# Rows of the last two experts placed by TensorE, an earlier reload of the running sum, and stores on two queues, in a diffusion backbone layer

## The chip, the cores and the metric

One core of one Trainium2 chip runs the whole layer as one program. Times are device microseconds of one execution. A profiled execution gives the span, from the first to the last instruction, and the trace behind all rows shown here. The engines are TensorE (PE in the profile; PEld is its weight load), VectorE (DVE), ScalarE (ACT), GpSimd (POOL) and SyncE (SP, which only issues transfers here). A name with a q behind it (SPq) is the engine's instruction queue.

## The reference, cut to what matters

```python
x = x + mx[2] * yx                                     # first residual
x = x + mx[5] * hier_moe(modulate(x, norm2_g, ...))    # 16 experts, top 2 inside the top group
return rmsnorm(x, final_g)

def hier_moe(h, ...):          # t: 512 tokens x 1024
    gates = ...                # (512, 16), two entries of a row are not zero
    for e in range(16):
        he = silu(t @ w1[e]) * (t @ w3[e])             # 1024 -> 512, twice
        out = out + gates[:, e:e + 1] * (he @ w2[e])   # 512 -> 1024
```

All data are float32. A token goes to two of the 16 experts. The last step is a norm over the 1024 values of each token, scaled by `final_g`.

## The kernel before, in words

The experts take the second half of the time. For each of them up to 96 tokens (CAP) are gathered from a table `td` in DRAM by an indirect transfer of GpSimd's queue, turned by TensorE (`columns`), multiplied by w1 and w3 (`up_`), gated (`gated` on ScalarE, `hidden` on VectorE), turned again (`hidden_t`), multiplied by w2 (`down`), scaled by the gate (`rows`, on VectorE) and added to the tokens' rows of `yd`, a running sum in DRAM, by a scatter that adds (`add_rows`, an indirect transfer of GpSimd's queue). A part behind the main path, under `tc.If(nmax > CAP)`, repeats the work for experts with more than 96 tokens. It is not entered in this run.

Weights come in 192 pieces of 512 KB, 12 for an expert, into a ring of 34 slots. Each piece is split into two reduced parts, a high one (a copy by ScalarE) and a low one (a subtraction by VectorE that overwrites the slot), and each product is made of three (`mm3`). `used()` counts a piece as consumed, and issues the load 33 pieces ahead on SyncE and the split six pieces ahead on ScalarE and VectorE. The order of each engine's instructions is that of the program text (`manual_schedule`): every engine takes its own list in order and waits for the others by semaphores.

Expert 15 has no scatter. A 0/1 matrix that says which of its 96 rows belongs to which token is made on VectorE at expert 8 (`OH0`, four tiles of 128 tokens), turned by TensorE and kept as `oT`. At the end `final_parts` splits the scaled rows into a high and a low part, and `placed` multiplies them by `oT` into eight PSUM banks (four tiles of 128 tokens, two halves of 512 columns). `final_loads` reads the sum `yd` back into four tiles; `added` adds the banks to it (VectorE for tiles 0 to 2; for tile 3 TensorE adds the sum into the bank by a product with the identity). `squared` (ScalarE) sums the squares, `rooted` and `root` make the factor for two tiles at a time, `done` scales, and `store` writes a half tile as two transfers of 64 partitions, since a tile holds rows of two runs of the output. For tiles 0 to 2 the product with `final_g` is made by GpSimd (`by_g`), and `done` multiplies by the factor alone. The reads of `final_loads` stand in the program behind the scatter of expert 14, which they need. The slots that the last norm uses (`fr`) are those of the ring that would come after the last piece.

Nine products on a spare bank (`mm(bank[7]...)`) stand in TensorE's list between the placing and the additions of tile 3. The table for the square root is loaded by a small ScalarE instruction (`warm`) ahead of the last products.

Of the kernel before, what the change touches and what calls it, by code (L numbers as in the profile page):

```python
# [9 lines left out]
BF = mybir.dt.bfloat16  # L10
# [4 lines left out]
CAP = 96  # L15
# [3 lines left out]
def layer_kernel(  # L19
# [18 lines left out]
    def dap(t, off, dims):  # L38
        return bass.AP(tensor=t.tensor, offset=t.offset + off, ap=dims)
# [26 lines left out]
    def atr(kb, shape, part=128):  # L66
        return at(kb, shape, part, F32R)

    def f32(a):
        return a.bitcast(F32)  # L70
# [11 lines left out]
    def nb(g="w"):  # L82
        b = bank[groups[g][bctr[g] % len(groups[g])]]
        bctr[g] += 1
        return b
# [4 lines left out]
    def mm(o, l, r, start, stop):  # L90
        T.matmul(o, l, r, start=start, stop=stop)  # L91
# [104 lines left out]
    def tr(o, i, n=None):  # L196
        n = i.partition_size() if n is None else n
        T.transpose(o, i, ident[0:n, 0:n])  # L198
# [1168 lines left out]
    def gated(e):  # L1367
        S.activation(at(sil, [512], part=CAP), st["h", e, 0][0:CAP], AF.Silu)  # L1368
# [27 lines left out]
    def rows(e, hs=(0, 1)):  # L1396
        if e < 0:
            return
        yb = st["y", e]
        yt = at(YO if e < 15 else XG, [1024], part=CAP)  # L1400
        for h in hs:
            r = slice(h * 512, h * 512 + 512)
            V.scalar_tensor_tensor(yt[:, r], yb[h][0:CAP], gate[:, e:e + 1], mx5[h][0:CAP], op0=OP.mult, op1=OP.mult)  # L1403
        if e < 15:
            add_rows(yt, idx[:, e:e + 1])


# [13 lines left out]
    ab = tables()  # L1421


    fr = [ring[(len(pieces) + q) % len(ring)] for q in range(12)]
    yL_ = [at(fr[q], [1024]) for q in range(4)]
    fg = at(fr[4], [1024])
    yH, yl = atr(fr[5], [1024], part=CAP), atr(fr[6], [1024], part=CAP)
    yf = [at(fr[8 + q], [1024]) for q in range(4)]
    ss3 = ct([128, 2, 4], F32, "ss3")
    rs3 = ct([128, 4], F32, "rs3")  # L1430
# [6 lines left out]
        for i in range(4):  # L1437
            D.dma_start(yL_[i], yd[i * 128:(i + 1) * 128, :])

    def final_parts(h):  # L1440
        yt, r = at(XG, [1024], part=CAP), half[h]
        S.activation(yH[:, r], yt[:, r], AF.Copy)
        V.tensor_sub(yl[:, r], yt[:, r], f32(yH[:, r]))

    def placed(h):
        for i in range(4):
            b = st["f", i, h] = nb()
            mm(b, oT[:, i], yH[:, half[h]], True, False)
            mm(b, oT[:, i], yl[:, half[h]], False, (i, h) not in by_pe)

    by_pe = ((3, 0), (3, 1))

# [8 lines left out]

    def squared(i, h):
        S.activation(at(fr[7], [512]), total(i, h), AF.Square, accum_out=ss3[:, h, i:i + 1])  # L1463

    def by_g(i, h):
        P.tensor_mul(yf[i][:, half[h]], yL_[i][:, half[h]], fg[:, half[h]])

    def rooted(q):

# [12 lines left out]

    def store(i, y, r):
        for j in range(2):
            D.dma_start(dap(out, (2 * i + j) * 1024 + r.start, [[8192, 64], [1, r.stop - r.start]]), y[j * 64:(j + 1) * 64, r])

    def done(i, h, e):
        r, c = half[h], slice(i, i + 1)
        if e is V:
            V.scalar_tensor_tensor(yf[i][:, r], total(i, h), rs3[:, c], fg[:, r], op0=OP.mult, op1=OP.mult)  # L1490
        elif e is D:
            V.tensor_scalar(yf[i][:, r], yf[i][:, r], rs3[:, c], None, op0=OP.mult)  # L1492
        elif e is S:
            S.activation(yf[i][:, r], yf[i][:, r], AF.Copy, scale=rs3[:, c])
        else:
            P.tensor_scalar(yf[i][:, r], yf[i][:, r], rs3[:, c], None, op0=OP.mult)
        store(i, yf[i], r)

    load_to(len(ring) - 1)
    oT = atr(195, [4, 128], part=CAP)  # L1500
    if True:
        split_to(AHEAD - 1)
        up_(0, 0, 0)
        used()
        up_(0, 0, 1)
        used()
        up_(0, 0, 2)
        slots(*ab)
        gather(1)
        counts()  # L1510
        used()
        up_(0, 0, 3)
        used()
        up_(0, 1, 0)
        gated(0)
        used()
        up_(0, 1, 1)
        used()
        up_(0, 1, 2)
        used()  # L1520
        up_(0, 1, 3)
        hidden(0)
        columns(1, 0)
        columns(1, 1)
        used()
        hidden_t(0)
        gather(2)
        down(0, 0)
        used()
        down(0, 1)  # L1530
        parts(1, 0)
        used()
        down(0, 2)
        parts(1, 1)
        used()
        down(0, 3)
        used()
        up_(1, 0, 0)
        used()
        up_(1, 0, 1)  # L1540
        used()
        up_(1, 0, 2)
        used()
        for e in range(1, 14):
            if e == 8:
                for i in range(4):
                    V.tensor_scalar(OH0[i], slotI, RM[:, i, 15:16], None, op0=OP.is_equal)
            up_(e, 0, 3)
            columns(e + 1, 0)
            used()  # L1550
            columns(e + 1, 1)
            gather(e + 2)
            up_(e, 1, 0)
            rows(e - 1)
            gated(e)
            used()
            up_(e, 1, 1)
            used()
            parts(e + 1, 0)
            up_(e, 1, 2)  # L1560
            used()
            parts(e + 1, 1)
            up_(e, 1, 3)
            hidden(e)
            used()
            up_(e + 1, 0, 0)
            used()
            up_(e + 1, 0, 1)
            hidden_t(e)
            used()  # L1570
            up_(e + 1, 0, 2)
            used()
            down(e, 0)
            used()
            down(e, 1)
            used()
            down(e, 2)
            used()
            down(e, 3)
            used()  # L1580
            if e == 8:
                b = nb()
                for i in range(4):
                    tr(b[0:CAP, i * 128:(i + 1) * 128], OH0[i])
                S.activation(oT.rearrange("p a b -> p (a b)"), b[0:CAP], AF.Copy)
        up_(14, 0, 3)
        columns(15, 0)
        used()
        columns(15, 1)
        gather(16)  # L1590
        up_(14, 1, 0)
        rows(13)
        gated(14)
        used()
        up_(14, 1, 1)
        used()
        parts(15, 0)
        up_(14, 1, 2)
        used()
        parts(15, 1)  # L1600
        up_(14, 1, 3)
        hidden(14)
        used()
        up_(15, 0, 0)
        used()
        up_(15, 0, 1)
        hidden_t(14)
        used()
        up_(15, 0, 2)
        used()  # L1610
        down(14, 0)
        used()
        down(14, 1)
        used()
        up_(15, 0, 3)
        used()
        up_(15, 1, 0)
        gated(15)
        used()
        up_(15, 1, 1)  # L1620
        used()
        up_(15, 1, 2)
        used()
        up_(15, 1, 3)
        hidden(15)
        n_used[0] += 1
        down(14, 2)
        hidden_t(15)
        n_used[0] += 1
        down(14, 3)  # L1630
        rows(14)
        used()
        S.activation(warm, ones_f[0:1, 0:1], AF.Sqrt)
        final_loads()
        after(D.dma_start(fg, dap(final_g, 0, [[0, 128], [1, 1024]])), loads[-1], "the weights come first")
        for k in range(4):
            down(15, k, (0,))
        rows(15, (0,))
        final_parts(0)
        for k in range(4):  # L1640
            down(15, k, (1,))
        placed(0)
        rows(15, (1,))
        final_parts(1)
        placed(1)
        added(0, 0)
        squared(0, 0)
        by_g(0, 0)
        added(0, 1)
        squared(0, 1)  # L1650
        by_g(0, 1)
        for _ in range(9):
            mm(bank[7][:, 0:512], ones_b, ones_f.bitcast(BF)[:, None, 0:256].to_broadcast([128, 2, 256]), True, True)
        added(3, 0)
        added(3, 1)
        added(1, 0)
        squared(1, 0)
        by_g(1, 0)
        added(1, 1)
        squared(1, 1)  # L1660
        added(2, 0)
        squared(2, 0)
        by_g(2, 0)
        rooted(0)
        added(2, 1)
        squared(2, 1)
        by_g(2, 1)
        root(0)
        done(0, 0, D)
        done(1, 0, D)  # L1670
        squared(3, 0)
        squared(3, 1)
        done(0, 1, D)
        done(1, 1, V)
        rooted(1)
        root(1)
        done(2, 0, D)
        done(2, 1, S)
        done(3, 1, V)
        done(3, 0, V)  # L1680

    order_.__exit__(None, None, None)


    nmax = nc.values_load(cntI[0:1, 16:17], min_val=0, max_val=512)
    with tc.If(nmax > CAP):
        add_rows(at(XG, [1024], part=CAP), idx[:, 15:16])
        ini = at(YO, [6, 16, 4], part=CAP, dt=I32)
        P.memset(ini, 0)
# [102 lines left out]
```

## Time and profile before

| | |
|---|---|
| median of 3 runs | 679.98 us (676.18, 679.98, 684.03) |
| the profiled execution's own time | 677.51 us |
| its span | 675.8 us |
| TensorE, matmul | 611.0 us busy, 90% of the span |
| VectorE | 512.1 us, 76% |
| ScalarE | 349.2 us, 52% |
| GpSimd | 113.0 us, 17% |
| mean granted TensorE clock | 0.936 of full speed |
| DMA | 172.25 MB, 255 GB/s over the span |

The profile's shares are means over stages that have different limits, so the last 80 us are read by themselves: the windows give the busy time of each engine in a stretch, the chain of waits gives what released each step, and the timeline gives each instruction with its start and duration. The profiled execution is one execution; the three timed runs differ among each other by 7.85 us.

### The profile page before, as it was taken

How to read it: one execution, taken by the hardware profiler on the slowest of the kernel's cores; microseconds unless marked ns; L12 is line 12 of the kernel's file. 1: busy time of each engine (PE TensorE's matmuls, PEld its weight loads, DVE VectorE, ACT ScalarE, POOL GpSimd, SP SyncE). 2: the span in 40 equal slices, each digit the busy share in tenths (PEclk: the TensorE clock that was granted, in tenths of full speed). 3: DMA queues.
4: the chain of work that ended last, by engine and by line, in shares of the span. 5: the costliest groups of instructions: out<-in, count | busy, mean ns of one | idle time of the engine just before them, and what ended most of it. 6: DMA issues, size and time to landing. Idle time of an engine off the chain costs nothing.

```text
span 675.8 us, 9072 instructions
## 1 busy us (share of the span) xinstructions
PE 611.0 (90%) x3048; PEld 439.0 (65%) x3049; DVE 512.1 (76%) x836; ACT 349.2 (52%) x488; POOL 113.0 (17%) x103
## 2 busy tenths in 40 slices
PE   4779979999989998999795999999999999999980
PEld 2438846667746675888673777777777777777740
DVE  3586759868586344468856899999999999999854
ACT  3556512532221145054053777777777777778641
POOL 1011120020320100004101111222224322221023
PEclk9688999999989999799767999999999999999985
DMA  5996293545795539724698999999999999997055
GB/s 168 257 335 184 80 212 123 181 127 171 212 238 180 210 86 278 288 98 144 279 379 298 310 358 368 368 371 371 368 370 376 372 367 378 372 364 237 16 180 126
DMA packets 75081, 172.25 MB, mean 255 GB/s; under 512 B 6951, under 2 KB 27651, under 8 KB 75031
## 3 DMA queue, kind: packets, MB, share of 16 engines
q1 hardware_dynamic: 69400, 155.23, 66.6%
q0 software_dynamic: 5136, 16.35, 10.5%
q8 instruction: 25, 0.41, 0.2%
q14 instruction: 25, 0.20, 0.1%
q10 hardware_dynamic: 495, 0.06, 0.1%
HBM read 156.53 MB, written 14.02 MB: 252 GB/s over the span
## 4 chain that ended last, share of the span: by engine, by line
PE 76%; DMA 11%; DVE 5%; ACT 3%; SPq 2%; issue 1%; POOL 0%; POOLq 0%; DVEq 0%; ACTq 0%
PE bank L97 59%; PE bank L91 12%; DMA b<-in_w_mod_dram 6%; PE bank L198 4%; DMA b<-td,idx 1%; DMA b<-in_s_b_re_dram 1%; DMA b<-in_expert_w_dram 1%; SPq L164 1%; DMA b<-in_ctx_dram 1%; DVE rst L206 1%; ACT b L680 1%; DVE b L75 1%; DMA b<-yd 1%; DVE b L1492 0%; ACT b L1463 0%
## 5 line engine op out<-in xcount | busy, mean ns | idle before, releaser
L97 PE MATMUL bank<-b,b 128*96 128x512 f32 (+2 forms) x1872 | 449.4, 397 | 2.4 <-DVE b L1276 0.9
L97 PEld LDWEIGHTS bank<-b,b 128*96 128x96 f32 (+1 forms) x1872 | 319.1, 175 | 117.9 <-issue 7.5
L75 DVE TENSOR_TENSOR b<-b,b 128x1024 fp32r<-128x1024 f32 (+2 forms) x246 | 268.1, 1136 | 41.3 <-ACT b L74 40.8
L74 ACT ACTIVATE b<-b 128x1024 fp32r<-128x1024 f32 (+2 forms) x246 | 234.3, 990 | 49.8 <-DVE b L992 22.3
L198 PE MATMUL bank<-ident,b 96*128 96x96 f32 (+3 forms) x323 | 46.6, 286 | 26.1 <-DMA b<-td,idx 7.2
L198 PEld LDWEIGHTS bank<-ident,b 96*128 96x128 f32 (+3 forms) x323 | 43.2, 186 | 36.2 <-issue 8.3
L1247 POOL DMA_INDIRECT yd<-b,idx x15 | 51.2, 3412 | 41.7 <-DVE b L1403 41.4
L1242 POOL DMA_INDIRECT b<-td,idx x15 | 16.2, 1082 | 211.9 <-PE bank L198 162.8
L91 PE MATMUL bank<-b,b 128*64 128x96 f32 (+7 forms) x384 | 50.8, 372 | 0.3
L74 ACT ACTIVATE b<-bank 128x384 fp32r<-128x384 f32 x46 | 22.0, 479 | 45.4 <-PE bank L198 45.4
L91 PEld LDWEIGHTS bank<-b,b 128*64 128x64 f32 (+3 forms) x376 | 30.0, 145 | 18.9 <-issue 12.9
L864 ACT ACTIVATE b<-bank 128x512 f32<-128x512 f32 x8 | 4.8, 597 | 69.9 <-PE bank L91 69.9
L75 DVE TENSOR_TENSOR b<-bank,b 128x384 fp32r<-128x384 f32 x46 | 25.4, 553 | 12.4 <-ACT b L74 12.4
L91 PE MATMUL bank<-b,sc 128*32 128x512 f32 x128 | 21.3, 627 | 6.2 <-DMA b<-in_w_mod_dram 6.2
L1403 DVE SCALAR_TENSOR_TENSOR b<-bank,gate,b 96x512 f32<-96x512 f32 x32 | 22.5, 741 | 1.3 <-PE bank L97 1.3
L1174 POOL TENSOR_TENSOR b<-b,b 128x1024 f32<-128x1024 f32 x4 | 9.3, 2356 | 81.2 <-DVE b L1124 81.2
L875 ACT ACTIVATE b<-bank 128x512 f32<-128x512 f32 x6 | 3.6, 597 | 29.5 <-PE bank L91 29.5
L91 PE MATMUL bank<-OH,b 128*128 128x96 f32 x64 | 15.2, 439 | 0.7 <-DVE OH L1228 0.7
L91 PEld LDWEIGHTS bank<-OH,b 128*128 128x128 f32 x64 | 15.0, 330 | 0.8 <-DVE OH L1228 0.8
L91 PEld LDWEIGHTS bank<-b,sc 128*32 128x32 f32 x128 | 3.1, 108 | 18.3 <-DMA b<-in_w_mod_dram 9.5
L1368 ACT ACTIVATE b<-bank 96x512 f32<-96x512 f32 x16 | 9.5, 592 | 7.7 <-PE bank L97 7.7
L1274 ACT ACTIVATE b<-bank,AST 128x96 f32<-128x96 f32 x4 | 1.4, 429 | 21.7 <-PE bank L91 21.7
(334 smaller groups left out, 431.7 us busy)
## 6 DMA issues: line engine op xcount, KB each, us to landing
b<-in_expert_w_dram SPq DMA_DIRECT2D x192, 512.0 KB
b<-in_w_mod_dram SPq DMA_DIRECT2D x48, 512.0 KB
b<-in_w_in_dram SPq DMA_DIRECT2D x20, 512.0 KB
b<-in_x_dram SPq DMA_DIRECT2D x16, 256.0 KB
b<-in_w_out_dram SPq DMA_DIRECT2D x16, 256.0 KB
yd<-b SPq DMA_DIRECT2D x8, 256.0 KB
td<-b SPq DMA_DIRECT2D x4, 512.0 KB
b<-yd SPq DMA_DIRECT2D x4, 512.0 KB
```

Source lines behind the costliest of these rows:

```text
L74: S.activation(hi, x_, AF.Copy)
L75: return (e or V).tensor_sub(lo, x_, f32(hi))
L91: T.matmul(o, l, r, start=start, stop=stop)
L97: T.matmul(o, l, r, start=start and n == 0, stop=stop and n == 2)
L164: D.dma_start(t, dap(w_in, off, [[2560, 128], [2560 * 128, 8], [1, 128]]))
L198: T.transpose(o, i, ident[0:n, 0:n])
L206: V.tensor_scalar(v[i], ss, 4.0 ** -i / 1024, 4.0 ** -i * 1e-6, op0=OP.mult, op1=OP.add)
L1174: P.tensor_mul(XA[i], XR[i], accp[2])
L1242: return P.indirect_dma_start(out=xg, out_offset=None, in_=td[:, :], in_offset=bass.IndirectOffsetOnAxis(ap=idx[:, e:e + 1], axis=0), boun ...
L1247: P.indirect_dma_start(out=yd[:, :], out_offset=bass.IndirectOffsetOnAxis(ap=ix, axis=0), in_=src, in_offset=None, bounds_check=639, oob_i ...
L1368: S.activation(at(sil, [512], part=CAP), st["h", e, 0][0:CAP], AF.Silu)
L1403: V.scalar_tensor_tensor(yt[:, r], yb[h][0:CAP], gate[:, e:e + 1], mx5[h][0:CAP], op0=OP.mult, op1=OP.mult)
```

## The change: what it does

1. Expert 14's rows are not scattered any more. A second 0/1 matrix is made for it (`places(14)`, four comparisons on VectorE, behind `rows(13)`), turned (`places_turned(14)`, four transposes and one ScalarE copy, under expert 15), its scaled rows are split (`final_parts(14, ...)`), and `placed` sums four products for each bank, two of each expert, in place of two.
2. `final_loads` and the load of `final_g` are issued under expert 15, behind the first product of its w1, in place of behind its gating. The last scatter that they wait for is now that of expert 13.
3. In the last norm the GpSimd products are gone; each scaling is one VectorE instruction with both factors. The order of additions, squares, roots and scalings is another one, and the nine products on the spare bank are gone.
4. A tile is stored when both halves are scaled, as two transfers of 64 partitions by 4 KB, one issued by SyncE and one by ScalarE.
5. In the part that is not entered, expert 14's rows are scattered as well.

```diff
--- before.py
+++ after.py
@@ -1401,7 +1401,7 @@
         for h in hs:
             r = slice(h * 512, h * 512 + 512)
             V.scalar_tensor_tensor(yt[:, r], yb[h][0:CAP], gate[:, e:e + 1], mx5[h][0:CAP], op0=OP.mult, op1=OP.mult)
-        if e < 15:
+        if e < 14:
             add_rows(yt, idx[:, e:e + 1])
 
 
@@ -1421,10 +1421,11 @@
     ab = tables()
 
 
-    fr = [ring[(len(pieces) + q) % len(ring)] for q in range(12)]
+    fr = [ring[(len(pieces) + q) % len(ring)] for q in range(15)]
     yL_ = [at(fr[q], [1024]) for q in range(4)]
     fg = at(fr[4], [1024])
-    yH, yl = atr(fr[5], [1024], part=CAP), atr(fr[6], [1024], part=CAP)
+    yH, yl = ([atr(fr[q], [1024], part=CAP) for q in p] for p in ((12, 5), (13, 6)))
+    oT = [atr(q, [4, 128], part=CAP) for q in (fr[14], 195)]
     yf = [at(fr[8 + q], [1024]) for q in range(4)]
     ss3 = ct([128, 2, 4], F32, "ss3")
     rs3 = ct([128, 4], F32, "rs3")
@@ -1437,16 +1438,28 @@
         for i in range(4):
             D.dma_start(yL_[i], yd[i * 128:(i + 1) * 128, :])
 
-    def final_parts(h):
-        yt, r = at(XG, [1024], part=CAP), half[h]
-        S.activation(yH[:, r], yt[:, r], AF.Copy)
-        V.tensor_sub(yl[:, r], yt[:, r], f32(yH[:, r]))
+    def final_parts(e, h):
+        yt, r = at(YO if e < 15 else XG, [1024], part=CAP), half[h]
+        S.activation(yH[e - 14][:, r], yt[:, r], AF.Copy)
+        V.tensor_sub(yl[e - 14][:, r], yt[:, r], f32(yH[e - 14][:, r]))
+
+    def places(e):
+
+        for i in range(4):
+            V.tensor_scalar(OH0[i], slotI, RM[:, i, e:e + 1], None, op0=OP.is_equal)
+
+    def places_turned(e):
+        b = nb()
+        for i in range(4):
+            tr(b[0:CAP, i * 128:(i + 1) * 128], OH0[i])
+        S.activation(oT[e - 14].rearrange("p a b -> p (a b)"), b[0:CAP], AF.Copy)
 
     def placed(h):
         for i in range(4):
             b = st["f", i, h] = nb()
-            mm(b, oT[:, i], yH[:, half[h]], True, False)
-            mm(b, oT[:, i], yl[:, half[h]], False, (i, h) not in by_pe)
+            for e in range(2):
+                mm(b, oT[e][:, i], yH[e][:, half[h]], e == 0, False)
+                mm(b, oT[e][:, i], yl[e][:, half[h]], False, e == 1 and (i, h) not in by_pe)
 
     by_pe = ((3, 0), (3, 1))
 
@@ -1461,9 +1474,6 @@
 
     def squared(i, h):
         S.activation(at(fr[7], [512]), total(i, h), AF.Square, accum_out=ss3[:, h, i:i + 1])
-
-    def by_g(i, h):
-        P.tensor_mul(yf[i][:, half[h]], yL_[i][:, half[h]], fg[:, half[h]])
 
     def rooted(q):
 
@@ -1482,22 +1492,17 @@
 
     def store(i, y, r):
         for j in range(2):
-            D.dma_start(dap(out, (2 * i + j) * 1024 + r.start, [[8192, 64], [1, r.stop - r.start]]), y[j * 64:(j + 1) * 64, r])
+            (D, S)[j].dma_start(dap(out, (2 * i + j) * 1024 + r.start, [[8192, 64], [1, r.stop - r.start]]),
+                                y[j * 64:(j + 1) * 64, r])
 
     def done(i, h, e):
         r, c = half[h], slice(i, i + 1)
         if e is V:
             V.scalar_tensor_tensor(yf[i][:, r], total(i, h), rs3[:, c], fg[:, r], op0=OP.mult, op1=OP.mult)
-        elif e is D:
-            V.tensor_scalar(yf[i][:, r], yf[i][:, r], rs3[:, c], None, op0=OP.mult)
-        elif e is S:
-            S.activation(yf[i][:, r], yf[i][:, r], AF.Copy, scale=rs3[:, c])
-        else:
-            P.tensor_scalar(yf[i][:, r], yf[i][:, r], rs3[:, c], None, op0=OP.mult)
-        store(i, yf[i], r)
+        if h:
+            store(i, yf[i], slice(0, 1024))
 
     load_to(len(ring) - 1)
-    oT = atr(195, [4, 128], part=CAP)
     if True:
         split_to(AHEAD - 1)
         up_(0, 0, 0)
@@ -1543,8 +1548,7 @@
         used()
         for e in range(1, 14):
             if e == 8:
-                for i in range(4):
-                    V.tensor_scalar(OH0[i], slotI, RM[:, i, 15:16], None, op0=OP.is_equal)
+                places(15)
             up_(e, 0, 3)
             columns(e + 1, 0)
             used()
@@ -1579,10 +1583,7 @@
             down(e, 3)
             used()
             if e == 8:
-                b = nb()
-                for i in range(4):
-                    tr(b[0:CAP, i * 128:(i + 1) * 128], OH0[i])
-                S.activation(oT.rearrange("p a b -> p (a b)"), b[0:CAP], AF.Copy)
+                places_turned(15)
         up_(14, 0, 3)
         columns(15, 0)
         used()
@@ -1590,6 +1591,7 @@
         gather(16)
         up_(14, 1, 0)
         rows(13)
+        places(14)
         gated(14)
         used()
         up_(14, 1, 1)
@@ -1603,7 +1605,10 @@
         used()
         up_(15, 0, 0)
         used()
+        final_loads()
+        after(D.dma_start(fg, dap(final_g, 0, [[0, 128], [1, 1024]])), loads[-1], "the weights come first")
         up_(15, 0, 1)
+        places_turned(14)
         hidden_t(14)
         used()
         up_(15, 0, 2)
@@ -1631,59 +1636,48 @@
         rows(14)
         used()
         S.activation(warm, ones_f[0:1, 0:1], AF.Sqrt)
-        final_loads()
-        after(D.dma_start(fg, dap(final_g, 0, [[0, 128], [1, 1024]])), loads[-1], "the weights come first")
         for k in range(4):
             down(15, k, (0,))
+        final_parts(14, 0)
+        final_parts(14, 1)
         rows(15, (0,))
-        final_parts(0)
+        final_parts(15, 0)
         for k in range(4):
             down(15, k, (1,))
         placed(0)
         rows(15, (1,))
-        final_parts(1)
+        final_parts(15, 1)
+        added(3, 0)
+        for i in range(3):
+            added(i, 0)
+            squared(i, 0)
+        squared(3, 0)
         placed(1)
-        added(0, 0)
-        squared(0, 0)
-        by_g(0, 0)
-        added(0, 1)
-        squared(0, 1)
-        by_g(0, 1)
-        for _ in range(9):
-            mm(bank[7][:, 0:512], ones_b, ones_f.bitcast(BF)[:, None, 0:256].to_broadcast([128, 2, 256]), True, True)
-        added(3, 0)
         added(3, 1)
-        added(1, 0)
-        squared(1, 0)
-        by_g(1, 0)
-        added(1, 1)
-        squared(1, 1)
-        added(2, 0)
-        squared(2, 0)
-        by_g(2, 0)
-        rooted(0)
-        added(2, 1)
-        squared(2, 1)
-        by_g(2, 1)
+        for i in range(3):
+            added(i, 1)
+            squared(i, 1)
+            if i == 1:
+                rooted(0)
         root(0)
-        done(0, 0, D)
-        done(1, 0, D)
-        squared(3, 0)
         squared(3, 1)
-        done(0, 1, D)
+        done(0, 0, V)
+        done(0, 1, V)
+        rooted(1)
+        done(1, 0, V)
+        root(1)
         done(1, 1, V)
-        rooted(1)
-        root(1)
-        done(2, 0, D)
-        done(2, 1, S)
+        done(3, 0, V)
         done(3, 1, V)
-        done(3, 0, V)
+        done(2, 0, V)
+        done(2, 1, V)
 
     order_.__exit__(None, None, None)
 
 
     nmax = nc.values_load(cntI[0:1, 16:17], min_val=0, max_val=512)
     with tc.If(nmax > CAP):
+        add_rows(at(YO, [1024], part=CAP), idx[:, 14:15])
         add_rows(at(XG, [1024], part=CAP), idx[:, 15:16])
         ini = at(YO, [6, 16, 4], part=CAP, dt=I32)
         P.memset(ini, 0)
```

## Rows read from the trace of the kernel before

**Rows 1.** Windows (us): length, each engine's busy us and instructions; clock; DMA share, GB/s.

```profile
613.00:619.00 6.00, 6.00 (x32) 4.50 (x31) 6.00 (x7) 4.78 (x6) 0.00 (x0) 1.00 0.89 359
619.00:630.00 11.00, 11.00 (x52) 7.75 (x51) 10.19 (x13) 8.10 (x10) 3.30 (x1) 1.00 0.27 47
```

**Rows 2.** Chain of waits from 640 us: start, us, what.

```profile
646.55 1.75 PE bank L91 x8
648.30 3.46 DMA b<-yd
...
652.58 0.73 ACT b L1463 x2
...
665.10 0.30 ACT rs L1472
...
667.21 0.88 DVE b L1490 x2
```

**Rows 3.** Who waited for whom, SyncE: us in total, times, longest.

```profile
SPq L1438 <- DMA yd<-b,idx: 34.7, 1, 34.7
```

**Rows 4.** Timeline from 619 us: start, us, engine, line, operation; idle before and releaser.

```profile
619.99 3.30 POOL L1247 DMA_INDIRECT yd<-b,idx  x1 [14.61 <-DVE b L1403]
...
642.30 2.16 POOL L1247 DMA_INDIRECT yd<-b,idx  x1 [19.01 <-DVE b L1403]
642.38 0.20 ACT L1633 ACTIVATE warm<-ones_f 1x1 f32<-1x1 f32 x1
...
660.34 11.67 SPq L1485 DMA_DIRECT2D out_dram<-b  x16
```

**Rows 5.** Windows of one or two us: old stores, x loads, td stores, scatter.

```profile
661.00:662.00 1.00, 0.00 (x0) 0.00 (x0) 0.54 (x1) 0.00 (x0) 1.00 (x2) 0.68 0.50 104
667.00:668.00 1.00, 0.00 (x0) 0.00 (x0) 1.00 (x2) 0.00 (x0) 0.00 (x0) 0.50 0.96 201
...
673.00:674.00 1.00, 0.00 (x0) 0.00 (x0) 0.00 (x0) 0.00 (x0) 0.00 (x0) 0.50 0.30 68
252.00:253.00 1.00, 1.00 (x6) 0.84 (x5) 1.00 (x1) 0.00 (x0) 0.00 (x0) 1.00 1.07 246
334.00:336.00 2.00, 2.00 (x11) 2.00 (x10) 1.96 (x2) 0.00 (x0) 0.00 (x0) 0.50 1.02 404
...
645.00:646.00 1.00, 1.00 (x6) 0.72 (x5) 0.69 (x1) 0.22 (x1) 0.00 (x0) 1.00 1.14 106
```

**Rows 6.** Timeline at expert 8, the matrix for expert 15.

```profile
509.20 0.81 DVE L1547 TENSOR_SCALAR OH<-slotI,RM 128x96 f32<-128x96 f32 x4
...
526.20 0.60 ACT L1585 ACTIVATE b<-bank 96x512 fp32r<-96x512 f32 x1 [0.99 <-PE bank L198]
```

**Rows 7.** Timeline at expert 14: its gated product, its transposes.

```profile
623.96 0.68 DVE L1372 TENSOR_TENSOR b<-b,bank 96x512 f32<-96x512 f32 x1
...
626.04 0.53 PEld L198 LDWEIGHTS bank<-ident,b 96*128 96x128 f32 x4
```

**Rows 8.** Timeline behind expert 15's products: gating, copy, subtraction.

```profile
643.80 0.75 DVE L1403 SCALAR_TENSOR_TENSOR b<-bank,gate,b 96x512 f32<-96x512 f32 x1 [0.65 <-PE bank L97]
...
647.37 0.63 ACT L1442 ACTIVATE b<-b 96x512 fp32r<-96x512 f32 x1 [2.15 <-DVE b L1403]
648.03 0.69 DVE L1443 TENSOR_TENSOR b<-b,b 96x512 fp32r<-96x512 f32 x1 [0.70 <-ACT b L1442]
```

**Rows 9.** Timeline of the last norm: additions, tile 3 on TensorE, scalings.

```profile
651.86 2.50 DVE L1457 TENSOR_TENSOR b<-b,bank 128x512 f32<-128x512 f32 x4 [3.14 <-DMA b<-yd]
...
656.07 2.90 PE L91 MATMUL bank<-b,ident 128*128 128x512 f32 x4
...
661.46 2.87 DVE L1492 TENSOR_SCALAR b<-b,rs 128x512 f32<-128x512 f32 x2 [1.15 <-POOL b L1466]
664.25 0.74 DVE L1490 SCALAR_TENSOR_TENSOR b<-b,rs,b 128x512 f32<-128x512 f32 x1
...
666.29 0.49 DVE L1492 TENSOR_SCALAR b<-b,rs 128x512 f32<-128x512 f32 x1
```

## The prediction, made before the changed kernel was run

> **What bounds the kernel now.** I read four views in this order. First the windows over the last experts: TensorE is busy in every microsecond at a granted clock of 1.00 (the higher level, 2.4 GHz), while the weights have arrived by about 619 us, after which DMA moves 47 GB/s [rows 1]. So until the last product of expert 15 only work on TensorE's own path costs time. The same rows show the one thing to fear there: VectorE is busy 6.00 of 6.00 us from 613 to 619 us. Second, the chain of waits from 640 us: products until 646.55 us, then those that place expert 15's rows, then 3.46 us of waiting for the running sum to be read back, then VectorE, ScalarE and GpSimd in turn until 668.09 us [rows 2]. Third, who waits: SyncE stood 34.7 us before the read-back, waiting for a scatter [rows 3]. That was expert 14's, issued at 642.30 us; the one of expert 13 left at 619.99 us [rows 4]. Fourth, single microseconds around the stores: at 667 to 668 us the DMA engines are 0.96 busy at only 201 GB/s, and the data end 0.3 us into the slice 673 to 674 [rows 5]. The span is 675.8 us, so 2.5 us follow the last data.
>
> Everything after 646.55 us, 29.2 us, is tail. The change works there, and pays with a little inside the experts.
>
> **Step 1, under experts 14 and 15.** VectorE gets four comparisons; the same four for expert 15 took 0.81 us together [rows 6]. They fall into the stretch in which VectorE is full. If each of its instructions behind them moves by 0.81 us, the gated product of expert 14 ends at 625.45 instead of 624.64, and its transposes need it at 626.04 [rows 7]. The cover is thin but there; without it TensorE would lose at most the 0.81 us, and ScalarE's new copy (0.60 us, [rows 6]) could add as much. TensorE itself gets four transposes; four load in 0.53 us [rows 7], partly under their neighbours. I take +0.4 us, bounds 0 and +1.5. The reads of the sum (four DMAs) and of the last norm's weights now stand on SyncE's queue from about 625 us. No load waits behind them, since SyncE had already come to them 34.7 us before 648.3 [rows 3]. They need expert 13's scatter: expert 14's had landed 6 us after its issue (642.30 to 648.30, [rows 2, 4]), so 626 us, or 632 if the queue is slower. Then 2.6 MB take some 6.5 us at the 404 GB/s of another transfer with rows of 4 KB [rows 5]. They land near 635 to 640, ten microseconds before use. Expert 14's scatter leaves GpSimd's queue at no loss, as nothing but the read-back waited for it.
>
> **Step 2, the start of the additions: 651.86 to 649.4.** ScalarE is done with the square-root table at 642.58 [rows 4], 643.0 with step 1. Then expert 14's rows are copied (2 x 0.63) and subtracted on VectorE (2 x 0.69), until 645.0; the gating of expert 15's first half (0.75) follows, where it started at 643.80 before, then its copy and subtraction: 647.1. Second half: 0.75, 0.63, 0.69, with handoffs 649.4 [rows 8]. The read-back, which was waited for, is there; late next is VectorE itself. Gain 2.4 us, bounds 1.5 and 3.1 (it could start at 648.72, where its last subtraction ended before).
>
> **Step 3, from the first addition to the last scaled row: 16.2 to 13.9 us.** TensorE places two experts, 32 products instead of 16, at 1.75/8 = 0.219 us [rows 2], from 646.95. First half until 650.45; then tile 3 is added by TensorE: two such additions made four records of 2.90 us together at clocks between the two levels [rows 9], so one costs at most 1.45 us, and as two records no less than two products, 0.44; I take 0.9, as TensorE no longer idles before it. Second half 651.35 to 654.85, its first tile at 652.25. VectorE adds three tiles (2.50/4 = 0.625 each, [rows 9]) until 651.3, waits for TensorE, and adds two more until 653.9. ScalarE squares at 0.75 us each [rows 2] from 650.1: the sixth ends at 654.65 and frees the first root. The second root of before took 1.2 us from its ScalarE part to the scaling behind it (665.10 to 666.29, [rows 2, 9]), and an addition of 0.62 falls between: 656.45. Then eight scalings on VectorE at 0.72 us (0.74 alone, [rows 9]), 5.8, and what of the second root VectorE does itself, 1.1: 663.3. Before, two scalings took 2.87 us beside GpSimd's products and waited 1.15 us for them; one took 0.49 without [rows 9]. Gain 2.3 us, bounds 1.0 and 3.0 (ScalarE's own store issue, some 0.7 us a store on SyncE [rows 4], stands in front of its second square root, which has 0.4 us of room).
>
> **Step 4, the stores: 7.7 to 5.4 us.** Before, 16 stores of 64 partitions x 2 KB left SyncE one by one over 11.67 us [rows 4]; the data ended last, not the last scaling. Now 8 stores of 64 x 4 KB leave from two queues, the first pair at 658.0, the last at 663.3. First data came some 1.1 us after the first issue (660.34, then a slice half busy, [rows 4, 5]). What two half-tile transfers at once reach, no row shows. From below: the x loads, also 64 partitions x 4 KB, on one queue: 246 GB/s at a share of 1.07. From above: stores of all 128 partitions, 404 GB/s at 1.02 [rows 5]. I take 300: the engines were as busy at 246 as at 404, so something on the half-tile side holds them, and two different halves at once should hold them less. Then 2.1 MB need 7.0 us from 659.1, and the last 0.52 MB 1.75 us from 664.4: both end at 666.1, and with 2.5 us behind, the span at 668.7. At 404 GB/s it would be 668.2, at 246 670.1, at the 201 GB/s of the old stores 672.0.
>
> The Trainium skill speaks against this part: "SBUF — State Buffer", section "Can I just issue two DMAs to hit both halves?", says that two transfers to different halves run on the same 16 engines and together gained only 6%, whichever engines issue them. By that rule (an estimate: 246 x 1.06 = 260 GB/s) the span would end near 669.7. The rows, all of one queue, neither confirm nor exclude it.
>
> **Sum.** Step 1 is inside step 2's start. 2.4 + 2.3 + 2.3 = 7.0 us off the profiled execution: its span of 675.8 becomes 668.8, its time of 677.51 becomes 670.5. The median of the three runs, 679.98 us, lies 2.5 above it; the same gain gives **672.9 us**.
>
> **The rivals.** *A, as forecast* (chance 0.50).
> *B, the stores stay as slow as one queue's* (0.29): half-tile transfers from two queues do not help each other. For it: shares of 0.96 to 1.07 at 201 to 246 GB/s, so SyncE's issuing was not what limited. Against: no row has both halves in flight from two queues. Price: a span of 670.1 to 672.0, a gain of 5.7 to 3.8; 674.3 to 676.2 us. The Trainium skill's section named above would have it so.
> *C, the reads are not early* (0.06), that is, the change does not do what it says: a dependence on a ring slot or on the sum keeps SyncE until about 648. Then the additions begin at about 652 again, 2.5 us lost: 675.4 us. For it: SyncE takes its queue in order and stood 34.7 us before. Against: by the code, the pieces in the reused slots are multiplied before the reads are issued.
> *D, VectorE starves TensorE* (0.10) in experts 14 and 15, since it is full from 613 us: all the 1.5 us of step 1 and the tail at its lower gains; 4 us left, 676 us. Against: the 0.6 us of cover in step 1.
> *E, slower than before* (0.05): the two store streams disturb each other. Place: after 659.1. Price: 2.1 MB at r GB/s; the end passes the old 675.8 when r is below 148, and counts as slower below 100. At 106 GB/s, the lowest that fully busy engines show (the scatter's slice, share 1.14, [rows 5]), the span ends at 681.4 and the time is 685.6. Against: no plain transfer with busy engines in these rows fell below 201 GB/s.
>
> **Numbers.** Less than 1% (6.8 us) can't be told from no change. A itself spans 671.5 to 674.5, its gain of 7.0 on the edge of that bound: two thirds of it count as faster (0.33), and a quarter of B with the scatter of the runs (0.08); E's worse half is slower (0.03), the rest is within 1%. Faster 0.41, same 0.56, slower 0.03. The range takes in A, B, C and D, and below A half the distance from the runs' median to their lowest: 668.5 to 677.
>
> **What would show it.** Right: TensorE without a gap from expert 14 to about 655.8 at clock 1.00; reads landed before 645; first addition at 649 to 650; last scaling near 663; near 300 GB/s or more in the stores, and a span end some 5.4 us behind the last scaling. Wrong: an idle piece of TensorE between 619 and 629 (D); a wait on the reads (C); DMA fully busy at 200 to 250 GB/s until 667 or later (B). The forecast also fails if VectorE waits somewhere in the tail that I have as back to back, above all between the two roots.

## The result and the profile after

The changed kernel takes 671.71 us (median of 20 runs, 669.49 to 680.77) against 679.23 us of the kernel before (20 runs, 675.57 to 684.03). The ratio is 0.9896, 95% interval 0.9874 to 0.9919: faster by 1.0%, with an interval that reaches to both sides of the 1% that the prediction set as the least that can be told from no change. In a second set of 12 runs, on another occasion, it was 0.9937 (0.9905 to 0.9969). The profiled execution has a span of 668.2 us and took 669.96 us.

The spans of two single executions should not be subtracted here. The row that counts GpSimd's scatters tells why: it names the start of the first one, which is where the experts get under way. In the kernel before:

```profile
L1247 POOL DMA_INDIRECT yd<-b,idx x15: 2079/3311/5622, 386.2 to 642.3; - x15
```

and in the changed one (columns: line, engine, operation, count, shortest, median and longest in ns, first and last start):

```profile
L1247 POOL DMA_INDIRECT yd<-b,idx x14: 2079/3313/5622, 384.5 to 618.3; - x14
```

The changed kernel came to its first scatter 1.7 us earlier, in a part that the change does not touch. Over the fourteen traces of this document that start lies anywhere between 384.1 and 392.0 us, while from it to the turning of expert 15's input every one of them takes 230.7 to 230.8 us. So I read every kernel from its first scatter to the end of the span (289.6 us before, 283.7 after), and inside that from the end of expert 15's last product, 646.55 us before and 645.30 after; the rest is called the tail. The gain that does not depend on the first half is 5.9 us, 0.45 us lost under the experts and 6.35 won in the tail.

The chain of waits after (start, us, what), to be held against [rows 2]:

```profile
645.29 6.38 PE bank L91 x26
...
651.70 0.70 DVE b L1470
...
654.89 1.42 DVE b L1501 x2
...
659.25 2.06 DVE b L1501 x3
```

TensorE's placing is now the first 6.4 us of the tail, the 3.46 us of waiting for the read-back are gone, and VectorE ends the chain at 661.32 us without GpSimd. The instructions behind it, from the timeline:

```profile
617.91 0.80 DVE L1449 TENSOR_SCALAR OH<-slotI,RM 128x96 f32<-128x96 f32 x4
618.27 5.62 POOL L1247 DMA_INDIRECT yd<-b,idx  x1 [14.61 <-DVE b L1403]
...
622.97 0.67 DVE L1372 TENSOR_TENSOR b<-b,bank 96x512 f32<-96x512 f32 x1
...
624.89 0.42 PEld L198 LDWEIGHTS bank<-ident,b 96*128 96x128 f32 x4
...
627.73 1.75 SPq L1439 DMA_DIRECT2D b<-yd  x4
...
645.33 0.75 DVE L1403 SCALAR_TENSOR_TENSOR b<-bank,gate,b 96x512 f32<-96x512 f32 x1
...
647.39 1.87 DVE L1470 TENSOR_TENSOR b<-b,bank 128x512 f32<-128x512 f32 x3
...
648.78 1.02 PE L91 MATMUL bank<-b,ident 128*128 128x512 f32 x2
...
649.24 4.24 PE L91 MATMUL bank<-b,b 96*128 96x512 f32 x16
...
650.77 0.69 DVE L1470 TENSOR_TENSOR b<-b,bank 128x512 f32<-128x512 f32 x1 [1.51 <-PE bank L91]
...
656.33 5.48 SPq L1495 DMA_DIRECT2D out_dram<-b  x4
...
659.91 1.41 DVE L1501 SCALAR_TENSOR_TENSOR b<-b,rs,b 128x512 f32<-128x512 f32 x2
```

Expert 13's scatter leaves at 618.27, the reads at 627.73, 20 us ahead of the first addition at 647.39 (651.86 before, [rows 9]). The windows (columns as in [rows 1]) show that TensorE never idles for it and that the reads have the DMA engines to themselves; the last four rows are stretches of the stores:

```profile
619.00:630.00 11.00, 11.00 (x54) 7.86 (x53) 10.32 (x12) 8.29 (x12) 4.89 (x1) 1.00 0.36 67
630.00:636.00 6.00, 6.00 (x27) 4.17 (x26) 6.00 (x6) 4.46 (x5) 0.00 (x0) 1.00 0.96 381
...
658.00:659.00 1.00, 0.00 (x0) 0.00 (x0) 1.00 (x3) 0.00 (x0) 0.00 (x0) 1.00 0.92 188
...
660.00:661.00 1.00, 0.00 (x0) 0.00 (x0) 1.00 (x2) 0.00 (x0) 0.00 (x0) 0.50 1.09 201
...
662.00:663.00 1.00, 0.00 (x0) 0.00 (x0) 0.00 (x0) 0.00 (x0) 0.00 (x0) 0.50 1.04 352
...
665.00:666.00 1.00, 0.00 (x0) 0.00 (x0) 0.00 (x0) 0.00 (x0) 0.00 (x0) 0.50 0.18 70
```

With stores from two queues in flight the DMA engines are still 0.92 to 1.09 busy at 188 to 201 GB/s, as in [rows 5], until the backlog of the last tiles raises the rate to 352 at the same busy share.

### The profile page after: what moved, and what is told of

Its sections match the earlier page's. It is cut to its first block, busy times and chain, and to the rows that moved or that the text cites. A ratio compares the mean times of both kernels' runs of the same rounds, so it can differ in the third digit from the quotient of the medians.

```text
span 668.2 us, 9076 instructions
## 1 busy us (share of the span) xinstructions
PE 608.8 (91%) x3059; PEld 440.3 (66%) x3060; DVE 512.8 (77%) x843; ACT 350.1 (52%) x490; POOL 106.4 (16%) x97
## 4 chain that ended last, share of the span: by engine, by line
PE 76%; DMA 10%; DVE 8%; ACT 3%; issue 1%; SPq 0%; ACTq 0%; DVEq 0%
PE bank L97 59%; PE bank L91 11%; PE bank L198 5%; DMA b<-in_expert_w_dram 3%; DMA b<-in_w_mod_dram 3%; DMA b<-td,idx 1%; DMA b<-in_x_dram 1%; DMA b<-in_s_lambda_im_dram 1%; DVE b L1414 1%; DVE rst L206 1%; DVE b L1501 1%; ACT b L680 1%; DVE b L75 1%; DMA b<-in_b_mod_dram 1%; PE bank L1144 0%
## 5 line engine op out<-in xcount | busy, mean ns | idle before, releaser
L91 PE MATMUL bank<-b,b 128*64 128x96 f32 (+7 forms) x400 | 54.7, 372 | 0.2
L91 PEld LDWEIGHTS bank<-b,b 128*64 128x64 f32 (+3 forms) x392 | 33.6, 146 | 17.1 <-issue 10.7
```

## The experiments

Each kernel is read from its own trace. Columns: end of expert 15's products; from there the start of the additions, the end of the last scaling, the last data (to a quarter of a us) and the tail; first scatter to the end of the span; ratio to the kernel before, run beside it, with its interval. All in us.

| kernel | products end | additions | last scaling | last data | tail | scatter to end | ratio |
|---|---|---|---|---|---|---|---|
| before | 646.55 | 5.31 | 21.54 | 27.0 | 29.25 | 289.6 | |
| after | 645.30 | 2.09 | 16.02 | 20.2 | 22.90 | 283.7 | 0.9896 (0.9874 to 0.9919) |
| e1 after again | 649.20 | 2.08 | 16.02 | 20.2 | 22.90 | 283.6 | 0.9937 (0.9905 to 0.9969) |
| e2 placing alone | 651.97 | 2.09 | 16.63 | 23.9 | 26.13 | 286.9 | 0.9979 (0.9949 to 1.0009) |
| e3 norm and stores alone | 652.34 | 5.56 | 22.81 | 26.9 | 29.66 | 290.0 | 1.0007 (0.9981 to 1.0033) |
| e4 stores alone | 648.90 | 5.31 | 22.27 | 26.7 | 29.20 | 289.5 | 1.0001 (0.9977 to 1.0025) |
| e5 one queue | 647.16 | 2.09 | 15.90 | 20.5 | 23.24 | 284.0 | 0.9931 (0.9903 to 0.9958) |
| e6 half rows | 644.90 | 2.09 | 16.23 | 19.8 | 22.30 | 283.1 | 0.9925 (0.9896 to 0.9954) |
| e7 late reads | 646.92 | 2.09 | 16.02 | 20.3 | 23.08 | 283.9 | 0.9893 (0.9855 to 0.9931) |
| e8 GpSimd products | 645.90 | 2.09 | 17.03 | 22.0 | 24.30 | 285.0 | 0.9941 (0.9915 to 0.9966) |
| e9 whole tiles | 645.06 | 2.09 | 15.93 | 18.8 | 21.34 | 282.1 | 0.9891 (0.9856 to 0.9927) |
| e10 whole tiles, halves | 647.05 | 2.09 | 15.92 | 18.2 | 20.95 | 281.7 | 0.9898 (0.9862 to 0.9933) |
| e11 as e3, tile 3 last | 646.95 | 5.68 | 19.50 | 23.8 | 26.55 | 286.9 | 0.9947 (0.9919 to 0.9975) |
| e12 as e10, tile 3 last | 645.25 | 2.10 | 15.25 | 17.8 | 20.25 | 281.0 | 0.9843 (0.9800 to 0.9885) |

**e1, the changed kernel again.** No edit.

> The changed kernel once more, for a second trace on this chip. The tail (end of expert 15's last product to the end of the span) was 29.3 us before and 22.9 after. If the tail's gain is fixed and the rest of the difference is chance further up, the tail is 22.9 +- 0.3 us again, whatever the start of expert 14 comes to. Rival: the new tail varies from execution to execution, then it moves by more than 0.5 us.

The tail is 22.90 us again, while the products end 3.9 us later. One trace gives the tail to about 0.2 us (e7, whose instructions in the tail are the same, has 23.08); the ratios carry the chance of the first half as well.

**e2, the placing alone.**

The last norm has the order, the GpSimd products and the 16 stores of the kernel before; its nine products on the spare bank are left out.

```diff
-            (D, S)[j].dma_start(dap(out, ...
+            D.dma_start(dap(out, ...
...
-        added(3, 0)
-        for i in range(3):
+        placed(1)
+        added(0, 0)
+        squared(0, 0)
+        by_g(0, 0)
...
-        done(0, 0, V)
+        done(0, 0, D)
```

> Only the placing: expert 14 placed by TensorE and the reads early as in the changed kernel, but the additions, GpSimd products, scalings and 16 single-queue stores of before (the nine products on the spare bank left out). My theory: the read-back wait of 3.1 us goes and additions start 2 to 3 us earlier, 0.9 to 1.7 us of it is lost again to the 16 more products, and the stores at 200 GB/s set the end: tail 26 to 27.5 us against 29.3 before. Rival: GpSimd and the 16 stores give it all back: 29 us.

26.13 us, as expected: additions at 2.09, and the last scaling only 0.6 us behind that of the changed kernel, yet the data end 3.7 us later, behind 16 stores on one queue, which move about 200 GB/s for as long as they run:

```profile
657.32 3.76 POOL L1479 TENSOR_TENSOR b<-b,b 128x512 f32<-128x512 f32 x3 [1.07 <-DVE b L1470]
...
664.07 10.23 SPq L1498 DMA_DIRECT2D out_dram<-b  x16
```

```profile
673.10:674.10 1.00, 0.00 (x0) 0.00 (x0) 0.00 (x0) 0.00 (x0) 0.00 (x0) 0.50 0.96 205
```

SyncE issues them nearly back to back, one every 0.64 us. Each moves 131 KB, so they leave at 205 GB/s, which is also the rate of the data.

**e3, norm and stores alone.** Expert 14 is scattered again, and the reads stand at their old place.

```diff
-        if e < 14:
+        if e < 15:
             add_rows(yt, idx[:, e:e + 1])
...
-        places(14)
...
-        places_turned(14)
...
-        final_parts(14, 0)
-        final_parts(14, 1)
...
-            for e in range(2):
+            for e in (1,):
```

> Only the norm and the stores: expert 14 scattered again as before, the reads in their old place, with the new order of the norm and the new stores. My theory: additions start 5.3 us behind the last product as before (2.1 us in the changed kernel), half of it hidden by 16 fewer products: tail 25 to 26 us. Rival, that the read-back was nearly hidden: 23 to 23.5 us.

A miss: 29.66 us, no gain at all. The waits (who for whom, us, times, longest) and the timeline name what took it:

```profile
PE bank L91 <- DMA b<-yd: 7.5, 1, 7.5
```

```profile
661.71 2.08 PE L91 MATMUL bank<-b,ident 128*128 128x512 f32 x2 [7.51 <-DMA b<-yd]
...
664.68 0.69 DVE L1470 TENSOR_TENSOR b<-b,bank 128x512 f32<-128x512 f32 x1 [3.53 <-PE bank L91]
```

In the new order TensorE adds tile 3, whose sum is read last, ahead of the placing of the second half. With late reads TensorE stands there, and VectorE waits 3.53 us for the second half behind it. e11 tests this.

**e4, the stores alone**, in the kernel before.

```diff
-            D.dma_start(dap(out, ...
+            (D, S)[j].dma_start(dap(out, ...
-        store(i, yf[i], r)
+        if (i, h) in ((0, 1), (1, 1), (2, 1), (3, 0)):
+            store(i, yf[i], slice(0, 1024))
```

> The kernel before with only the stores changed: whole tiles of 64 x 4 KB rows from two queues, when a tile's second half is scaled. Last scaling stays at 21.5 us behind the last product. If stores end 6.9 us behind the last scaling as in the changed kernel, the tail is 28.4 us (0.9 less than 29.3); if the two queues gave what I had forecast (5.4 us), 26.9; if they give nothing, 29.3 or more, since the first store starts 4 us later.

29.20 us: no gain beyond what one trace can tell. The last data come 4.4 us behind the last scaling (5.5 before), but the last scaling is 0.7 us later.

**e5, one queue.**

```diff
-            (D, S)[j].dma_start(dap(out, ...
+            D.dma_start(dap(out, ...
```

> The changed kernel with its 8 stores all on SyncE's queue. My theory (two queues help): data at 200 to 246 GB/s from 0.9 us after the first issue, so they end 0.5 to 2.5 us later than with two queues and the tail is 23.5 to 25.4 us. Rival B (half-tile transfers on two queues do not help each other): the tail stays at 22.9 within 0.3 us.

23.24 us, 0.34 more than with two queues, under my band and at the edge of rival B (0.3). The stores' windows:

```profile
659.40:660.40 1.00, 0.00 (x0) 0.00 (x0) 0.96 (x4) 0.00 (x0) 0.00 (x0) 1.00 1.04 201
...
663.40:664.40 1.00, 0.00 (x0) 0.00 (x0) 0.00 (x0) 0.00 (x0) 0.00 (x0) 0.50 0.94 303
...
666.40:667.40 1.00, 0.00 (x0) 0.00 (x0) 0.00 (x0) 0.00 (x0) 0.00 (x0) 0.50 0.76 270
```

From the first issue to the last data it takes 9.46 us (20.49 less 11.03 behind the products), against 9.12 with two queues: 4%, of which the chance of one trace can be half.

**e6, half rows**, still on two queues.

```diff
-        if h:
-            store(i, yf[i], slice(0, 1024))
+        store(i, yf[i], r)
```

> The changed kernel with its stores cut in half tiles as before (16 of 64 x 2 KB), still on two queues. If it is the row of 4 KB that makes the new stores faster (265 GB/s over all against 200), the data run at 200 GB/s again and the tail is 24 to 25 us. If it is the two queues, the rate stays and the earlier start gives the tail 22.4 to 23.2 us.

22.30 us. On two queues rows of 2 KB cost no rate:

```profile
657.00:658.00 1.00, 0.00 (x0) 0.00 (x0) 0.83 (x5) 0.04 (x1) 0.00 (x0) 0.50 0.94 328
...
663.00:664.00 1.00, 0.00 (x0) 0.00 (x0) 0.00 (x0) 0.00 (x0) 0.00 (x0) 0.50 0.96 277
```

and the first store leaves 0.7 us earlier. Waiting for whole tiles, as the change does, costs 0.6 us. One queue with rows of 2 KB is the only pairing that stays near 200 GB/s to its end (before, e2); longer rows (e5) or a second queue (e6) alone lift it.

**e7, the reads at their old place in the text.**

```diff
         used()
-        final_loads()
-        after(D.dma_start(fg, ...
         up_(15, 0, 1)
...
         S.activation(warm, ones_f[0:1, 0:1], AF.Sqrt)
+        final_loads()
+        after(D.dma_start(fg, ...
```

> The changed kernel with the reads of the sum and of the norm's weights at their old place in the program text, behind expert 15's gating. My theory: nothing else stands on SyncE's queue there, so they leave at the same moment, when expert 13's scatter has landed; tail 22.9 +- 0.3 us, and the reads some 10 us ahead of expert 15's last product. Rival: the place in the text counts, the reads leave near the last product and the tail grows by 2 to 3 us.

```profile
619.90 5.62 POOL L1247 DMA_INDIRECT yd<-b,idx  x1 [14.61 <-DVE b L1403]
...
629.34 1.75 SPq L1439 DMA_DIRECT2D b<-yd  x4
```

The reads leave 9.44 us after expert 13's scatter, as in the changed kernel (618.27 to 627.73, 9.46). Tail 23.08. The move in the text is worth nothing; what made the reads early is that expert 14's scatter is gone.

**e8, GpSimd's products back.**

```diff
+        if i < 3:
+            V.tensor_scalar(yf[i][:, r], yf[i][:, r], rs3[:, c], None, op0=OP.mult)
...
             squared(i, 0)
+            by_g(i, 0)
...
             squared(i, 1)
+            by_g(i, 1)
```

These are six products. The kernel before had five: it left the second half of tile 1 to VectorE.

> The changed kernel with GpSimd's six products by the norm's weights put back for tiles 0 to 2, and VectorE scaling those by the factor alone. If GpSimd's products slow VectorE beside them (1.43 us a scaling before, 0.49 without), additions and scalings lengthen and the tail is 24.5 to 27 us. Rival: with scalings of 0.49 in place of 0.72 us VectorE gains 1.4 us and the tail is 21.5 to 22.9.

24.30 us, 1.4 more, just under the band. The timeline of GpSimd (its spans are rough) and VectorE:

```profile
648.89 6.27 POOL L1479 TENSOR_TENSOR b<-b,b 128x512 f32<-128x512 f32 x5 [24.37 <-DVE b L1470]
...
653.87 1.32 DVE L1484 TENSOR_TENSOR ss<-ss 128x2 f32<-128x2 f32 x1 [0.85 <-ACT b L1476]
...
656.06 1.26 POOL L1479 TENSOR_TENSOR b<-b,b 128x512 f32<-128x512 f32 x1 [0.89 <-DVE rs L1491]
...
656.09 1.25 DVE L1492 TENSOR_TENSOR t<-rs 128x2 f32<-128x2 f32 x1
657.37 0.16 DVE L1493 TENSOR_TENSOR t<-t 128x2 f32<-128x2 f32 x1
...
657.84 0.88 DVE L1504 TENSOR_SCALAR b<-b,rs 128x512 f32<-128x512 f32 x2
```

It was not the scalings: they start at 657.84 us, when the last product has ended (657.32), and take 0.44 us each. It was instructions of two columns on the path to the first root, which took 1.32 and 1.25 us beside a GpSimd product, and 0.16 without. The Trainium skill, "SBUF — State Buffer", section "Who interferes with whom", has a rule that fits: a VectorE instruction with two inputs in SBUF contends with a GpSimd instruction that reads SBUF. The two rows of 1.32 and 1.25 us agree with it.

This run does not test scalings beside a GpSimd product. In the kernel before, two of them took 2.87 us beside products [rows 9].

**e9, whole tiles.** The last norm's tiles are numbered so that partition p of tile q holds token 4p + q; one store then takes all 128 partitions.

```diff
-            D.dma_start(yL_[i], yd[i * 128:(i + 1) * 128, :])
+            for b in range(2):
+                D.dma_start(yL_[i][b::2], yd[b * 256 + i * 64:b * 256 + i * 64 + 64, :])
...
-        S.activation(oT[e - 14].rearrange("p a b -> p (a b)"), b[0:CAP], AF.Copy)
+        S.activation(oT[e - 14].rearrange("p q (a b) -> p b q a", b=2), b[0:CAP].rearrange("p (b q a) -> p b q a", b=2, q=4), AF.Copy)
...
+        q = (S if i in (1, 3) else D)
+        q.dma_start(dap(out, i * 1024 + r.start, [[4096, 128], [1, r.stop - r.start]]), y[:, r])
...
```

> The changed kernel with the last norm's tiles numbered so that partition p of tile q holds token 4p + q: a tile is then stored by one transfer of all 128 partitions x 4 KB, two tiles by SyncE and two by ScalarE, and read by two transfers of 64 rows each into every second partition. My theory: the half-tile shape (64 partitions) is what holds the stores at some 250 GB/s; now 380 GB/s or more, last data 2.3 us behind the last scaling in place of 4.1, tail 20.6 to 21.4 us against 22.9. Rival: writes to the output run at 250 GB/s in any shape: tail 22.5 to 23.2.

21.34 us, and the rate is the one that was expected (the last data come 2.9 us behind the last scaling, 2.3 expected):

```profile
656.90:657.90 1.00, 0.00 (x0) 0.00 (x0) 0.90 (x6) 0.00 (x0) 0.00 (x0) 1.00 0.96 385
...
660.90:661.90 1.00, 0.00 (x0) 0.00 (x0) 0.08 (x1) 0.00 (x0) 0.00 (x0) 0.50 1.05 414
```

The first tile, alone in flight, runs at 385 GB/s, where as two half-tile transfers at once it ran at 188. The edit also brings the rows of a transfer nearer to each other in the output (16 KB apart, 32 before); that was not tested by itself.

**e10, the same in halves of the columns** (the edit of e6 on e9).

> As the kernel with whole-tile transfers, but each half of the columns is stored when it is scaled: 8 transfers of 128 partitions x 2 KB. If all partitions give the rate and the row of 2 KB costs nothing, the last transfer is half as long and the tail is 20.0 to 20.8 us. If a 2 KB row costs rate, 21.5 us or more.

20.95 us: 0.39 less than e9, and 0.15 past the upper edge of what I expected. With eight transfers, as many as the change has, the stores run at 379 to 381 GB/s from 662 to 664 us, so it is not the smaller number of transfers that makes e9 fast.

**e11, tile 3 last**, on e3.

```diff
-        added(3, 0)
         for i in range(3):
             added(i, 0)
             squared(i, 0)
-        squared(3, 0)
         placed(1)
+        added(3, 0)
         added(3, 1)
...
         root(0)
+        squared(3, 0)
         squared(3, 1)
```

> The kernel with expert 14 scattered again and the new norm, but TensorE's addition of tile 3 (and its squares) moved behind the placing of the second half. In the version with the old place TensorE stood 7.5 us at that addition, waiting for the last read, with the second half's placing queued behind it. If that wait is why norm and stores alone gained nothing, the second half's additions start 3 us earlier and the tail goes from 29.6 to 26 to 27.5 us. Rival: the late reads cost it anyway, tail 29 us or more.

```profile
655.20 1.88 DVE L1470 TENSOR_TENSOR b<-b,bank 128x512 f32<-128x512 f32 x3 [0.60 <-DMA b<-yd]
656.42 3.78 PE L91 MATMUL bank<-b,ident 128*128 128x512 f32 x4 [5.40 <-DMA b<-yd]
```

26.55 us. TensorE still waits 5.40 us for tile 3's sum, but nothing stands behind it; VectorE goes on with the second half as the reads land. So it was the order of two instructions that made norm and stores worth nothing without the early reads.

**e12, tile 3 last, on e10.**

> The kernel with whole-tile transfers in halves, with the same move of tile 3's addition and squares. The reads are early here, so only the 0.46 us of that addition and one square of 0.75 us leave the path to the first root: tail 20.0 to 20.6 us against 20.95. Rival: the second root becomes the later one and the tail stays at 20.9 or grows.

20.25 us, and 0.9843 (0.9800 to 0.9885) of the kernel before: the best version, 8.6 us shorter from the first scatter to the end than the kernel before and 2.7 shorter than the changed one. TensorE places both halves in one run:

```profile
645.09 7.44 PE L91 MATMUL bank<-b,b 96*128 96x512 f32 x32
```

and the chain of waits needs 5.47 us of it until VectorE takes over, against 6.38 in the changed kernel:

```profile
645.25 5.47 PE bank L91 x24
```

The two records fewer are tile 3's addition, which thus cost 0.91 us there, twice the 0.46 us between its first record and the next product that I had counted.

## Why the prediction was right, and where a size was off

The sum, 7.0 us, holds against the median (7.5 us over 20 runs each); against the part of the trace that repeats it is 1.1 us too large (5.9). From the median that the prediction started from, 679.98, a gain of 5.9 us gives 674.1, near the upper end of A (674.5) and 0.2 us short of the lower end of B (674.3): that the measured 671.71 lies well inside A is in part luck. Rounds of runs could not have told: their intervals allow 5.5 to 8.6 us in the first set and 2.1 to 6.4 in the second.

- **Step 1** (+0.4): from the eight transposes that turn expert 15's input to the end of the products it is 30.00 us after and 29.54 before, +0.46. TensorE has no gap, the gated product ends at 623.64 with TensorE's next need for it at 624.89: rival D did not come. Expert 13's scatter took 9.46 us from its start until SyncE went on, not 6, against ten microseconds of room; no harm.
- **Step 2** (additions 2.45 us behind the products): 2.09. Net of step 1 a gain of 2.8 us, 0.4 more than forecast. The sum let expert 14's copies push the gating of expert 15's second half back; it starts 0.04 us behind the products, before as after (646.59 and 645.33). Rival C did not come: before its reads SyncE waited 15.5 us for expert 13's scatter and 0.7 us for TensorE, and e7 shows that the place in the text does not matter.
- **Step 3** (13.9 us from the first addition to the last scaling): 13.93. The first scaling starts 9.6 us behind the products, 9.5 forecast. The one assumption in it, 0.9 us for tile 3's addition on TensorE, held: 0.91 us by the chains of e12 and the changed kernel. It is not hidden: VectorE waits 1.51 us for the second half, as forecast, and without the addition and a square in front (e12 against e10) the last scaling comes 0.67 us earlier. VectorE has no wait between the two roots. GpSimd's products, put back into the new order (e8), lengthen this stage by 1.0 us and the tail by 1.4, through the small instructions; what they cost in the old order, through the scalings that I had named, was not separated.
- **Step 4** (5.4 us from the last scaling to the end): 6.88, and 7.7 before. This is the term that was mis-sized, by 1.5 us: the 2.1 MB took some 8.1 us from the first data, about 260 GB/s on average, where I had taken 300 since "two different halves at once should hold them less". With rows of 4 KB two queues gave 4% (e5), on two queues 2 or 4 KB rows made no difference (e6), and all 128 partitions in one transfer gave 385 to 414 GB/s (e9). So my step from [rows 5] to two queues was wrong, and rival B's mechanism, at 0.29, was nearer. B's price was just missed, 5.7 us at most, since step 2 gave more, and its sign, full engines at 200 to 250 GB/s until 667, held for the first tiles only.

  Two things stay open. A tile alone in flight ran at 188 GB/s as two halves and at 385 as one transfer, yet the last tiles together reached 352 in the half-tile shape; why is not shown. And the busy share, from which I had ruled out that SyncE's issuing limits the old stores, does not tell: it was 0.92 at 188 GB/s and 1.04 at 352. One issue of 131 KB every 0.64 us (e2) fits their 200 GB/s as well, and e5 and e6, which each ease the issuing, both ran faster; no run tests it alone.

  The section of the Trainium skill cited with it, "Can I just issue two DMAs to hit both halves?", states 6% for two transfers and that all ports are reached only by one transfer over 128 partitions. e5 (4%, by one queue against two) and e9 agree with it; the 260 GB/s that the prediction worked out from it agrees with the average, but the backlog's 352 GB/s lies above it, and there the measurement decides.
- **Rival E** did not come: no microsecond of the stores from two queues with engines over 0.9 busy fell below 180 GB/s.

The parts do not add up by themselves: the placing alone gains 2.7 us from the first scatter to the end (e2), norm and stores alone lose 0.4 (e3), the stores alone gain 0.1 (e4), all together 5.9. The prediction took steps 3 and 4 as they are once the reads are early, and did not say that they hang on it. With tile 3 last, norm and stores gain 2.7 us without the early reads (e11), and the two parts then come to 5.4 of the 5.9.

## What to carry to other kernels

A last norm that waits for an accumulation in memory is best freed of the last accumulation itself, by work on an engine that has time; the place of the read in the program text then does not matter if its queue is empty. Before stores are spread over queues, ask how many partitions one transfer covers and how many bytes one issue moves: here one transfer over all partitions was worth 1.6 us (e9) and a second queue 0.3 (e5). A full busy share of the DMA engines did not mean a full rate. An instruction that waits for the last of several transfers belongs behind all work of its engine that does not.

## What the runs showed that was not expected

- The start of the first scatter moved by 8 us between executions of kernels that are alike up to there (384.1 to 392.0 us), while what follows repeated within 0.3 us (289.6 and 289.5 where the stores alone differ, 283.7, 283.6 and 283.9 in the changed kernel and its likes). TensorE's granted clock goes with it: from 200 to 300 us it was 0.92 in the two latest (e2 and e3, 391.2 and 392.0) and 0.95 to 0.97 in the others (384.1 to 388.6). What moved the clock was not followed up.
- An addition of 128 x 2 values took 1.32 us beside a GpSimd product, eight times its usual 0.16. In e2 an instruction with one input of that size took 1.20 us beside one as well (L1486), and 0.17 without.
- A store of 64 partitions took SyncE 0.47 us to issue, one of 128 partitions with twice the bytes 0.34.
